# A decoder layer on one Trainium2 core: norm chains spread by a share set by stage, one product of the seven moved first, and the last walk of the weights backwards

## Chip, cores and metric

One core of one Trainium2 chip. The metric is device time per launch in microseconds (us), the median of several runs. TensorE is called PE, VectorE DVE, ScalarE ACT, GpSimd POOL and SyncE SP, as in the profile.

## The reference, cut to what matters

One decoder layer runs over 1024 prompt tokens and 8 x 4 decode tokens, D = 1024, FFN width 2816:

```python
h = _rms(x, n_mix_pre)
z = h @ w_in                      # q, k, v, pooling input
a, k_state, v_state = attn_fn(q, k, v)        # window of 128 keys, sinks
m, pool_state = _pool_mixer(u, pool_prev, pos0, w_pool, pool_scale)
mix = jnp.concatenate([a, m], axis=-1) @ w_out
x = x + _rms(mix, n_mix_post)
f = _rms(x, n_ffn_pre)
f = (jax.nn.silu(f @ w_gate) * (f @ w_up)) @ w_down
x = x + _rms(f, n_ffn_post)
x = x + jax.nn.sigmoid(x @ w_ple_gate) * (p @ w_ple)
```

All of it is float32. The outputs are the new x of both token sets and the key, value and pooling states.

## The kernel before, in words

**Layout.** The 1056 tokens lie in three groups g = 0, 1, 2 of 352 columns; features lie on the 128 partitions, so D is eight chunks of 128, kept as two halves of four chunks (128x1408). A float32 product is done as three matmuls on high and low halves: `split` (L145 to L147) makes the high half with a cast on ACT and the low half (the names ending in l: wl, fl, sl, and the second half of hid and pl) with a subtraction on DVE; `gemm` (L248) multiplies high by high, high by low and low by high. All matmuls are issued by L117.

**Weights.** `w_load` (L151) fetches a weight tile through SP's queue into one of three raw buffers (wr), and `w_split` (L162) splits it into one of four pairs of tiles (wh, wl). A raw buffer is free when its low half is made, a pair when its last matmul has read it. `need` (L232) keeps up to five items ahead in a list, ITEMS, that is planned beforehand.

**The walk over the FFN.** The 22 chunks of the FFN width are taken as 11 slabs of two. WALK (L191) has 16 steps n: slabs 0 to 4 with group 2 alone, slabs 5 to 10 with all groups, slabs 0 to 4 again with groups 0 and 1 (steps 11 to 15). `gate_up` (L806) makes one chunk of silu(f·gate)·(f·up). Group 2 takes a direct product of 24 matmuls for gate and for up. Groups 0 and 1 share seven products of 12 matmuls instead of eight, in Strassen's manner: two with the gate weights and sums of x (B11, B21), then S2·T2, S3·T3, a quarter of the up weights times T4, S1·T1, S4·B22. The S are sums of the weights, made by `w_sums` (L780): four additions on POOL (L790) in place in the two raw buffers, after their own splits, and then a split of the results into sh and sl. `downs` (L921) multiplies a slab's hidden activations (hid) by the down weights, six matmuls an output, and is called after the first product or products of the next step.

**The norm chains.** What a norm needs is written as generators: `ffn_steps` (L700) for the norm behind the mixing sub-layer and the one ahead of the FFN, `ple_steps` (L894) for the norm behind the FFN, both with `rstd_steps` (L264), whose two small matmul groups sum the squares over the partitions (acc) and broadcast the reciprocal root (dg). Each yields a load, the matmuls' worth of DVE work in the piece, and a wait. `turn` (L678), called after each product, counts the matmuls issued and lets a chain go on to its next piece when its time has come; the next time is DVE's planned time plus load/share, share = 0.45. A smaller share spreads the pieces over more matmuls. `chain` starts a chain after a wait, `finish` runs chains to their end.

**What orders the engines.** From L755 PE's instructions keep the order in which they are written, chains' matmuls included. The other engines' order is made by the tile scheduler, so a piece that is emitted later need not stand later on DVE.

**The end.** `ple_out` (L938) makes one output chunk m of one group: 6 matmuls with the projection w_ple and 24 with w_ple_gate, a sigmoid, a product and a sum, then the store. Group 2 does m = 0 and 1 (FIRST = 2) ahead of the last slab's down products of groups 0 and 1, and m = 2 to 7 behind them; then a second walk over m = 0 to 7 does groups 0 and 1, and all weights are fetched and split again. `plan_ple` (L219) plans both walks.

Of the kernel before, what the change touches and what calls it, by code (L numbers as in the profile page):

```python
# [16 lines left out]
P = 128  # L17
D = 1024
KC = D // P
# [39 lines left out]
def trunk_kernel(  # L59
# [61 lines left out]
    def bank():  # L121
        return psum.tile([P, 512], F32, tag="b", name=nm("b"))
# [39 lines left out]
    def w_split(j):  # L162
        if j >= len(plan) or j in pairs:
            return
        w_load(j)
        shape = plan[j][1]
        hi, lo = w_tile(shape, "wh"), w_tile(shape, "wl")
        split(hi, lo, raws[j])
        pairs[j] = (hi, lo)
# [7 lines left out]
    def add_plan(src, shape):  # L177
        plan.append((src, shape))
        return len(plan) - 1
# [16 lines left out]
    def item(kind, *js):  # L196
        ITEMS.append((kind, js))
        return len(ITEMS) - 1

    def direct_item(src, shape):  # L200
        return item("direct", add_plan(src, shape))
# [15 lines left out]
    WPE = [[], []]  # L217

    def plan_ple(n, m):  # L219
        wp = direct_item(w_ple[m // 4], [P, 2, 512]) if m % 4 == 0 else WPE[n][-1][0]  # L220
        WPE[n].append((wp, direct_item(w_pg[m], [P, KC, P])))

    FIRST = 2
    for m in range(FIRST):
        plan_ple(0, m)
    WD[-1] = [direct_item(w_dn[WALK[-1][0], j], [P, SLAB, 512]) for j in range(2)]
    for m in range(FIRST, KC):
        plan_ple(0, m)
    for m in range(KC):
        plan_ple(1, m)  # L230

    made = {}  # L232

    def need(k, ahead=LOOK):

        for i in range(len(made), min(k + ahead + 1, len(ITEMS))):
            kind, js = ITEMS[i]
            if kind == "direct":
                w_split(js[0])
                made[i] = pairs[js[0]]  # L240
            else:
                made[i] = w_sums(*(raws[ITEMS[j][1][0]] for j in js))
            for kind, js in ITEMS[i + 1 : i + 3]:
                if kind == "direct":
                    w_load(js[0])
        return made[k]
# [61 lines left out]
    def bc4(r):  # L308
        return r.unsqueeze(1).to_broadcast([P, 4, r.shape[1]])
# [39 lines left out]
    n = 4 * NDEC * PST  # L349
# [83 lines left out]
    for c in range(4):  # L433
        n = NDEC * DSEQ
# [240 lines left out]
    now, dve = [0.0], [0.0]  # L675
    chains = []

    def turn(n, share=0.45):  # L678

        now[0] += n  # L680
        for ch in list(chains):
            while ch in chains and ch[1] <= now[0]:
                try:
                    load, wait = next(ch[0])
                except StopIteration:
                    chains.remove(ch)
                    break
                dve[0] = max(dve[0], now[0]) + load / share
                ch[1] = dve[0] + wait

    def chain(steps, wait=0):
        chains.append([steps, now[0] + wait])

    def finish(ch_list):
        for ch in ch_list:
            for _ in ch[0]:
                pass
            chains.remove(ch)

    def ffn_steps(g):  # L700

        r = yield from rstd_steps(acc[g])
        for yh, xh in zip(ys[g], x1[g]):
            ve.tensor_tensor(yh, yh, bc4(r), op=ALU.mult)
            ve.tensor_tensor(xh, xh, yh, op=ALU.add)
            se.activation(yh, xh, AF.Square)
            yield 20, 0
        yield 0, 13
        acc2 = sum_halves(ys[g], g)
        yield 20, 6  # L710
        r = yield from rstd_steps(acc2)
        for h in range(2):
            nc.sync.dma_start(x1d[g][h], x1[g][h])
            for c in range(4):
                k = 4 * h + c
                ve.scalar_tensor_tensor(  # L716
                    ys[g][h][:, c, :], x1[g][h][:, c, :], gn[:, 2, k : k + 1], r, op0=ALU.mult, op1=ALU.mult
                )
            yield 14, 0
            if (g, h) == (1, 0):  # L720
                t_sum("T1")
                yield 20, 0
            else:
                op = f_operand(ys[g][h], g)
                yield 10, 0
                if g == 2:
                    fs[2].append(op)
                else:
                    f7[f"B{h + 1}{g + 1}"] = op
        if g == 1:  # L730
            for name in ("T3", "T2", "T4"):
                t_sum(name)
                yield 20, 0
# [8 lines left out]
    f7 = {}  # L742
# [10 lines left out]
        f7[name] = f_operand(out, 0)  # L753

    pinned[0] = True  # L755
    chain(ffn_steps(2), 19)
    for m in range(4):
        for g in (0, 1):
            out_attn(m, g)
# [10 lines left out]
        turn(24)  # L770
    chain(ffn_steps(1), 19)
    finish(chains[:-2])


    hid = [None] * G
# [27 lines left out]
    def quarter(w, h):  # L803
        return tuple(t[:, 4 * h : 4 * h + 4, :] for t in w)

    def gate_up(items, slot, gs, pending):  # L806

        ig, iu, is_ = items
        n = N

        def product(w, x):
            ps = bank()
            gemm(ps[:, :n], ops4(w, x))
            turn(12)
            return ps[:, :n]

        def direct(w):
            ps = bank()
            gemm(ps[:, :n], ops8(w, fs[2]))
            turn(24)  # L820
            return ps[:, :n]

        def add(out, a, ps):
            ve.tensor_tensor(out, a, ps, op=ALU.add)

        wg = need(ig)
        if 0 in gs:
            p1 = tmp(n, "p1")
            se.copy(p1, product(quarter(wg, 0), f7["B11"]))
        if 2 in gs:  # L830
            sl = tmp(n, "sl")
            se.activation(sl, direct(wg), AF.Silu)
        if 0 in gs:
            c11 = tmp(n, "c11")
            add(c11, p1, product(quarter(wg, 1), f7["B21"]))
            se.activation(c11, c11, AF.Silu)
        if pending:
            pending()
        for g in gs:
            if slot == 0:  # L840
                hid[g] = half(g, F32R, "hid")
        wu = need(iu)
        if 2 in gs:
            ve.tensor_tensor(sl, sl, direct(wu), op=ALU.mult)
            hid_put(2, slot, sl)
        if 0 not in gs:
            return
        s = need(is_)
        add(p1, p1, product(s["S2"], f7["T2"]))
        u3 = tmp(n, "u3")  # L850
        add(u3, p1, product(s["S3"], f7["T3"]))
        c21 = tmp(n, "c21")
        add(c21, u3, product(quarter(wu, 1), f7["T4"]))
        ve.tensor_tensor(c21, c21, c11, op=ALU.mult)
        hid_put(0, slot, c21)
        p5 = product(s["S1"], f7["T1"])
        add(u3, u3, p5)
        add(p1, p1, p5)
        add(p1, p1, product(s["S4"], f7["B22"]))
        se.activation(p1, p1, AF.Silu)  # L860
        ve.tensor_tensor(u3, u3, p1, op=ALU.mult)
        hid_put(1, slot, u3)
# [31 lines left out]
    def ple_steps(g):  # L894

        pl = half(g, F32R, "pl")
        pls[g] = pl[:, 0:2, :], pl[:, 2:4, :]
        for k in range(2):
            pr = tmp(NS[g], "pr")
            nc.sync.dma_start(pr, p[:, k, OFF[g] : OFF[g + 1]])  # L900
            split(pl[:, k, :], pl[:, 2 + k, :], pr)
        x2s[g] = []
        for h in range(2):
            x2[g][h] = half(g, s="x2")
            nc.sync.dma_start(x2[g][h], x1d[g][h])
        r = yield from rstd_steps(acc3[g])
        for h in range(2):
            yh, xh = os_[g][h], x2[g][h]
            ve.tensor_tensor(yh, yh, bc4(r), op=ALU.mult)
            for c in range(4):  # L910
                k = 4 * h + c
                ve.scalar_tensor_tensor(  # L912
                    xh[:, c, :], yh[:, c, :], gn[:, 3, k : k + 1], xh[:, c, :], op0=ALU.mult, op1=ALU.add
                )
            yield 24, 0
            x2s[g].append(f_operand(xh, g))
            yield 10, 0
# [3 lines left out]
    def downs(n):  # L921
        s, gs = WALK[n]
        for m in range(KC):
            for g in (2, 0, 1):
                if g in gs:
                    (last_down if g == 2 and s == NSLAB - 1 else down)(n, m, g)
        if s == NSLAB - 1:
            chain(ple_steps(2), 19)

    for n, (s, gs) in enumerate(WALK):  # L930
        if n == AHEAD:
            finish(list(chains))
        for i in range(SLAB):
            gate_up(WGU[n][i], i, gs, (lambda: downs(n - 1)) if i == 0 and n else None)
    finish(list(chains))


    def ple_out(n, m, g):  # L938
# [15 lines left out]

    for m in range(FIRST):
        ple_out(0, m, 2)
# [5 lines left out]
    chain(ple_steps(1), 19)  # L962
    for m in range(FIRST, KC):
        ple_out(0, m, 2)
    finish(chains[:1])
    for m in range(KC):
        for g in (0, 1):
            if g == 1 and m == 0:
                finish(list(chains))
            ple_out(1, m, g)  # L970

# [86 lines left out]
```

## Time and profile before

| | before |
|---|---|
| median of 3 runs | 1228.29 us (1227.34 to 1229.78) |
| the profiled execution | 1225.98 us |
| its span (first to last instruction) | 1223.9 us |
| mean granted clock of PE | 0.971 |
| PE busy | 1147.9 us (94%) |
| DVE busy | 741.7 us (61%) |
| ACT busy | 433.3 us (35%) |
| POOL busy | 187.1 us (15%) |

The span is one execution, and all durations come from it. Busy shares are averages over stages with different limits. A wait is put down to the engine that released it last; the granted clock is that which the throttle left to PE.

### The profile page before, as it was taken

How to read it: one execution, taken by the hardware profiler on the slowest of the kernel's cores; microseconds unless marked ns; L12 is line 12 of the kernel's file. 1: busy time of each engine (PE TensorE's matmuls, PEld its weight loads, DVE VectorE, ACT ScalarE, POOL GpSimd, SP SyncE). 2: the span in 40 equal slices, each digit the busy share in tenths (PEclk: the TensorE clock that was granted, in tenths of full speed). 3: DMA queues.
4: the chain of work that ended last, by engine and by line, in shares of the span. 5: the costliest groups of instructions: out<-in, count | busy, mean ns of one | idle time of the engine just before them, and what ended most of it. 6: DMA issues, size and time to landing. Idle time of an engine off the chain costs nothing.

```text
span 1223.9 us, 17417 instructions
## 1 busy us (share of the span) xinstructions
PE 1147.9 (94%) x7099; PEld 1109.0 (91%) x7099; DVE 741.7 (61%) x1161; ACT 433.3 (35%) x755; POOL 187.1 (15%) x150
## 2 busy tenths in 40 slices
PE   4699999999889999999999999999969999999898
PEld 3599986779889999999999999999969999999798
DVE  6644245676487894534555555547866576679542
ACT  4222035656345552433131313123423223355220
POOL 3344012110000003102021111111112213200000
PEclk9599999999989999999999999999979999999899
DMA  6211130036235331202121211213212122246321
GB/s 231 67 35 47 52 115 18 18 114 217 69 139 167 131 120 35 73 32 70 35 70 35 63 41 35 70 35 99 81 52 69 41 98 70 64 132 245 105 70 42
DMA packets 35104, 101.11 MB, mean 83 GB/s; under 512 B 4148, under 2 KB 14676, under 8 KB 35024
## 3 DMA queue, kind: packets, MB, share of 16 engines
q1 hardware_dynamic: 33264, 98.22, 23.7%
q10 hardware_dynamic: 1760, 1.78, 0.5%
q8 instruction: 56, 0.92, 0.3%
q14 instruction: 24, 0.20, 0.1%
HBM read 89.87 MB, written 10.11 MB: 82 GB/s over the span
## 4 chain that ended last, share of the span: by engine, by line
PE 83%; DVE 8%; POOL 3%; ACT 3%; DMA 1%; issue 1%; POOLq 0%; SPq 0%; DVEq 0%; ACTq 0%
PE b L117 79%; POOL wr L790 3%; DVE wl L147 2%; PE b L541 1%; PE b L509 1%; DMA xr<-in_x_dram 1%; ACT wh L146 1%; DVE h L324 1%; DVE sl L147 1%; ACT a L483 1%; ACT sh L146 1%; DVE fl L147 1%; DVE y L716 0%; PE b L588 0%; DVE x L912 0%
## 5 line engine op out<-in xcount | busy, mean ns | idle before, releaser
L117 PE MATMUL b<-fh,wh 128*128 128x352 f32 x808 | 263.9, 327 | 10.8 <-ACT fh L146 10.8
L117 PE MATMUL b<-hid,wh 128*128 128x352 f32 x1056 | 255.7, 324 | 10.7 <-ACT hid L146 8.0
L117 PE MATMUL b<-fl,wh 128*128 128x352 f32 x808 | 261.4, 324 | 3.3 <-DVE fl L147 3.3
L146 ACT CAST wh<-wr 128x1024 fp32r<-128x1024 f32 x140 | 146.6, 1049 | 332.0 <-PE b L117 273.5
L117 PE MATMUL b<-fh,wl 128*128 128x352 f32 x808 | 261.2, 323 | 0.0
L147 DVE TENSOR_TENSOR wl<-wr,wh 128x1024 fp32r<-128x1024 f32 x140 | 176.7, 1263 | 65.9 <-ACT wh L146 65.7
L117 PEld LDWEIGHTS b<-hid,wh 128*128 128x128 f32 x1056 | 184.2, 189 | 13.0 <-ACT hid L146 8.8
L117 PE MATMUL b<-hid,wl 128*128 128x352 f32 x528 | 170.1, 322 | 0.0
L790 POOL TENSOR_TENSOR wr<-wr 128x512 f32<-128x512 f32 x44 | 60.3, 1370 | 682.9 <-DVE wl L147 482.0
L117 PEld LDWEIGHTS b<-fh,wh 128*128 128x128 f32 x808 | 153.1, 190 | 12.0 <-ACT fh L146 11.7
L117 PEld LDWEIGHTS b<-fl,wh 128*128 128x128 f32 x808 | 153.5, 190 | 4.8 <-DVE fl L147 4.4
L117 PEld LDWEIGHTS b<-fh,wl 128*128 128x128 f32 x808 | 153.4, 190 | 0.0
L880 DVE TENSOR_TENSOR o<-o,b 128x352 f32<-128x352 f32 x240 | 116.0, 515 | 43.0 <-PE b L117 42.9
L117 PE MATMUL b<-h,wh 128*128 128x352 f32 x480 | 123.7, 340 | 18.6 <-ACT wh L146 9.7
L117 PE MATMUL b<-fh,sh 128*128 128x352 f32 x352 | 114.8, 326 | 6.6 <-ACT sh L146 6.6
L117 PE MATMUL b<-fh,sl 128*128 128x352 f32 x352 | 114.0, 324 | 3.3 <-DVE sl L147 3.3
L117 PE MATMUL b<-fl,sh 128*128 128x352 f32 x352 | 113.5, 322 | 0.0
L117 PEld LDWEIGHTS b<-h,wh 128*128 128x128 f32 x480 | 88.5, 199 | 21.8 <-ACT wh L146 9.7
L147 DVE TENSOR_TENSOR sl<-wr,sh 128x1024 fp32r<-128x1024 f32 x44 | 53.7, 1223 | 85.8 <-ACT sh L146 85.8
L146 ACT CAST sh<-wr 128x1024 fp32r<-128x1024 f32 x44 | 45.9, 1045 | 152.3 <-POOL wr L790 109.1
L117 PEld LDWEIGHTS b<-hid,wl 128*128 128x128 f32 x528 | 99.8, 189 | 0.0
L117 PE MATMUL b<-h,wl 128*128 128x352 f32 x240 | 80.3, 335 | 2.5 <-DVE wl L147 2.5
(156 smaller groups left out, 1601.4 us busy)
## 6 DMA issues: line engine op xcount, KB each, us to landing
wr<-in_w_gu_dram SPq DMA_DIRECT2D x64, 512.0 KB, 3.2
wr<-in_w_dn_dram SPq DMA_DIRECT2D x32, 512.0 KB, 3.4
wr<-in_w_pg_dram SPq DMA_DIRECT2D x16, 512.0 KB, 3.9
wr<-in_w_in_dram SPq DMA_DIRECT2D x10, 512.0 KB, 3.3
xr<-in_x_dram SPq DMA_DIRECT2D x6, 704.0 KB, 5.2
x<-in_x_dram SPq DMA_DIRECT2D x6, 704.0 KB, 9.4
x1d<-x SPq DMA_DIRECT2D x6, 704.0 KB, 3.5
x<-x1d SPq DMA_DIRECT2D x6, 704.0 KB, 5.6
```

The lines of the kernel that those rows point to most:

```text
L117: ins = te.matmul(*args, **kw)
L146: se.copy(hi, src)
L147: ve.tensor_tensor(lo, src, hi.bitcast(F32), op=ALU.subtract)
L324: ve.scalar_tensor_tensor(lo[:, c, :], xr[:, c, :], gc, hi[:, c, :].bitcast(F32), op0=ALU.mult, op1=ALU.subtract)
L483: se.activation(t[:, c, :], t[:, c, :], AF.Exp, bias=nmx[:, c : c + 1], scale=scale, accum_out=sm[:, c : c + 1])
L509: te.matmul(which[kv][:, c * WIN : (c + 1) * WIN], qT[c][rows, b * WIN : (b + 1) * WIN], kT[rows, at * WIN : (at + 1) * WIN], start=True, ...
L541: te.matmul(o[64 * kv : 64 * kv + 64, :], vtok[:, at, 64 * kv : 64 * kv + 64], pt[:, 4 * kv : 4 * kv + 4, :], start=n == 0, stop=n == len( ...
L790: ge.tensor_tensor(out, a, b, op=op)
L880: ve.tensor_tensor(o, o, v, op=ALU.add)
```

## The change

- **Share by stage.** The share becomes a cell that is set as the program goes on: 0.6 from the first chain until groups 0 and 1 have left the output projection (it was 0.45), 0.45 in the FFN, 0.1 when group 2's per-layer chain starts (behind the down products of slab 10), 0.7 for the chains of groups 0 and 1 at the end. Group 2's FFN chain starts 8 matmuls after it is due instead of 19.
- **T4.** In walk steps 11 to 15 the product with T4 is issued ahead of S2 and S3, and added where it was.
- **The end.** FIRST is 1. The second walk runs m = 7 to 0 and reuses the pairs of m = 7 and 6, and of w_ple's second half, that the first walk left: three loads and three splits fewer. The `finish` in it moves to m = 7.

```diff
--- before.py
+++ after.py
@@ -220,14 +220,19 @@
         wp = direct_item(w_ple[m // 4], [P, 2, 512]) if m % 4 == 0 else WPE[n][-1][0]
         WPE[n].append((wp, direct_item(w_pg[m], [P, KC, P])))
 
-    FIRST = 2
+    FIRST = 1
     for m in range(FIRST):
         plan_ple(0, m)
     WD[-1] = [direct_item(w_dn[WALK[-1][0], j], [P, SLAB, 512]) for j in range(2)]
     for m in range(FIRST, KC):
         plan_ple(0, m)
-    for m in range(KC):
-        plan_ple(1, m)
+
+    WPE[1] = [None] * 6 + WPE[0][6:]
+    wp = WPE[0][-1][0]
+    for m in reversed(range(6)):
+        if m == 3:
+            wp = direct_item(w_ple[0], [P, 2, 512])
+        WPE[1][m] = wp, direct_item(w_pg[m], [P, KC, P])
 
     made = {}
 
@@ -675,7 +680,9 @@
     now, dve = [0.0], [0.0]
     chains = []
 
-    def turn(n, share=0.45):
+    share = [0.6]
+
+    def turn(n):
 
         now[0] += n
         for ch in list(chains):
@@ -685,7 +692,7 @@
                 except StopIteration:
                     chains.remove(ch)
                     break
-                dve[0] = max(dve[0], now[0]) + load / share
+                dve[0] = max(dve[0], now[0]) + load / share[0]
                 ch[1] = dve[0] + wait
 
     def chain(steps, wait=0):
@@ -753,7 +760,7 @@
         f7[name] = f_operand(out, 0)
 
     pinned[0] = True
-    chain(ffn_steps(2), 19)
+    chain(ffn_steps(2), 8)
     for m in range(4):
         for g in (0, 1):
             out_attn(m, g)
@@ -770,6 +777,7 @@
         turn(24)
     chain(ffn_steps(1), 19)
     finish(chains[:-2])
+    share[0] = 0.45
 
 
     hid = [None] * G
@@ -845,12 +853,16 @@
             hid_put(2, slot, sl)
         if 0 not in gs:
             return
+        if 2 not in gs:
+            p4 = product(quarter(wu, 1), f7["T4"])
         s = need(is_)
         add(p1, p1, product(s["S2"], f7["T2"]))
         u3 = tmp(n, "u3")
         add(u3, p1, product(s["S3"], f7["T3"]))
         c21 = tmp(n, "c21")
-        add(c21, u3, product(quarter(wu, 1), f7["T4"]))
+        if 2 in gs:
+            p4 = product(quarter(wu, 1), f7["T4"])
+        add(c21, u3, p4)
         ve.tensor_tensor(c21, c21, c11, op=ALU.mult)
         hid_put(0, slot, c21)
         p5 = product(s["S1"], f7["T1"])
@@ -925,6 +937,7 @@
                 if g in gs:
                     (last_down if g == 2 and s == NSLAB - 1 else down)(n, m, g)
         if s == NSLAB - 1:
+            share[0] = 0.1
             chain(ple_steps(2), 19)
 
     for n, (s, gs) in enumerate(WALK):
@@ -933,6 +946,7 @@
         for i in range(SLAB):
             gate_up(WGU[n][i], i, gs, (lambda: downs(n - 1)) if i == 0 and n else None)
     finish(list(chains))
+    share[0] = 0.7
 
 
     def ple_out(n, m, g):
@@ -963,9 +977,9 @@
     for m in range(FIRST, KC):
         ple_out(0, m, 2)
     finish(chains[:1])
-    for m in range(KC):
+    for m in reversed(range(KC)):
         for g in (0, 1):
-            if g == 1 and m == 0:
+            if g == 1 and m == KC - 1:
                 finish(list(chains))
             ple_out(1, m, g)
```

On DVE, where group 2 enters the FFN: acc are sums of squares, wl a weight's low half, L704 and L705 (L711 and L712 in the changed kernel) are group 0's y·r and x+y, L716 (L723) group 2's scalings y<-x,c,b, and fl are the low halves of group 2's normalised x, first half and second. Before:

```order
L608 TENSOR_TENSOR acc_1303<-acc_1303,sq_2809 128x352
L147 TENSOR_TENSOR wl_2813<-wr_2736,wh_2812 128x1024
L705 TENSOR_TENSOR x_2326<-x_2326,y_1266 128x1408
L716 SCALAR_TENSOR_TENSOR y_1268<-x_2322,c_72,b_2823 128x352 x4
L716 SCALAR_TENSOR_TENSOR y_2188<-x_2324,c_72,b_2823 128x352 x3
L147 TENSOR_TENSOR fl_2831<-y_1268,fh_2830 128x1408
L716 SCALAR_TENSOR_TENSOR y_2188<-x_2324,c_72,b_2823 128x352
L704 TENSOR_TENSOR y_2532<-y_2532,b_2818 128x1408
L147 TENSOR_TENSOR fl_2840<-y_2188,fh_2839 128x1408
L705 TENSOR_TENSOR x_2328<-x_2328,y_2532 128x1408
```

After:

```order
L723 SCALAR_TENSOR_TENSOR y_1268<-x_2322,c_72,b_2748 128x352 x3
L723 SCALAR_TENSOR_TENSOR y_2188<-x_2324,c_72,b_2748 128x352 x2
L147 TENSOR_TENSOR wl_2785<-wr_2701,wh_2784 128x1024
L613 TENSOR_TENSOR acc_1303<-acc_1303,sq_2781 128x352
L711 TENSOR_TENSOR y_1266<-y_1266,b_2794 128x1408
L147 TENSOR_TENSOR fl_2791<-y_1268,fh_2790 128x1408
L712 TENSOR_TENSOR x_2326<-x_2326,y_1266 128x1408
L613 TENSOR_TENSOR acc_1303<-acc_1303,sq_2825 128x352
L147 TENSOR_TENSOR wl_2829<-wr_2746,wh_2828 128x1024
L723 SCALAR_TENSOR_TENSOR y_2188<-x_2324,c_72,b_2748 128x352 x2
L711 TENSOR_TENSOR y_2535<-y_2535,b_2794 128x1408
L147 TENSOR_TENSOR fl_2840<-y_2188,fh_2839 128x1408
```

Six of group 2's eight scalings (one of them stands above these rows) and its first fl have moved ahead of x+y; y·r stays ahead of the first fl, and the second fl stays behind both pieces of group 0.

On DVE, in walk step 11, where two chunks' weights pass through the raw buffers: wl are low halves of weights and sl of weight sums, L824 (L832) sums of products, L861 (L873) u·p, L909 (L921) group 2's o·r and L912 (L924) its residual updates. wl_7728 (wl_7721) frees the raw buffer for the next gate or up weights. Before:

```order
L147 TENSOR_TENSOR sl_7606<-wr_7337,sh_7605 128x1024
L912 SCALAR_TENSOR_TENSOR x_7654<-o_3042,c_72,x_7654 128x352 x2
L147 TENSOR_TENSOR wl_7612<-wr_7485,wh_7611 128x1024
L912 SCALAR_TENSOR_TENSOR x_7654<-o_3042,c_72,x_7654 128x352 x2
L824 TENSOR_TENSOR p_7339<-p_7339,b_7702 128x352
L824 TENSOR_TENSOR c_7748<-p_7733,b_7749 128x352
L909 TENSOR_TENSOR o_3043<-o_3043,b_7715 128x1408
L861 TENSOR_TENSOR u_7631<-u_7631,p_7339 128x352
L824 TENSOR_TENSOR p_7733<-p_7733,b_7774 128x352
L912 SCALAR_TENSOR_TENSOR x_7656<-o_3043,c_72,x_7656 128x352
L147 TENSOR_TENSOR wl_7728<-wr_7609,wh_7727 128x1024
```

After:

```order
L147 TENSOR_TENSOR sl_7606<-wr_7337,sh_7605 128x1024
L873 TENSOR_TENSOR u_7667<-u_7667,p_7339 128x352
L832 TENSOR_TENSOR c_7741<-p_7726,b_7742 128x352
L147 TENSOR_TENSOR hid_7596<-u_7667,hid_7596 128x352
L147 TENSOR_TENSOR wl_7625<-wr_7485,wh_7624 128x1024
L921 TENSOR_TENSOR o_3042<-o_3042,b_7774 128x1408
L147 TENSOR_TENSOR wl_7721<-wr_7609,wh_7720 128x1024
L924 SCALAR_TENSOR_TENSOR x_7652<-o_3042,c_72,x_7652 128x352 x4
```

Of group 2's chain, both o·r and five updates stood ahead of wl_7728; one o·r stands ahead of wl_7721, and the updates behind it.

On DVE, some ten rows further in the same step, where the hid of group 1 (hid_7596) is finished ahead of the step's down products; L880 (L892) are sums of down products. Before:

```order
L912 SCALAR_TENSOR_TENSOR x_7656<-o_3043,c_72,x_7656 128x352 x2
L824 TENSOR_TENSOR p_7733<-p_7733,b_7840 128x352
L147 TENSOR_TENSOR sl_7868<-wr_7485,sh_7867 128x1024
L824 TENSOR_TENSOR c_7892<-p_7877,b_7893 128x352
L861 TENSOR_TENSOR u_7788<-u_7788,p_7733 128x352
L880 TENSOR_TENSOR o_4477<-o_4477,b_7912 128x352
L147 TENSOR_TENSOR fl_7952<-x_7656,fh_7951 128x1408
L147 TENSOR_TENSOR hid_7596<-u_7788,hid_7596 128x352
```

After:

```order
L147 TENSOR_TENSOR hid_7595<-c_7816,hid_7595 128x352
L832 TENSOR_TENSOR p_7726<-p_7726,b_7836 128x352
L147 TENSOR_TENSOR sl_7859<-wr_7485,sh_7858 128x1024
L873 TENSOR_TENSOR u_7801<-u_7801,p_7726 128x352
L832 TENSOR_TENSOR c_7883<-p_7868,b_7884 128x352
L892 TENSOR_TENSOR o_4477<-o_4477,b_7903 128x352
L147 TENSOR_TENSOR hid_7596<-u_7801,hid_7596 128x352
L924 SCALAR_TENSOR_TENSOR x_7654<-o_3043,c_72,x_7654 128x352 x2
```

Group 2's last fl and its last two updates stood ahead of hid_7596; the updates now stand behind it and the fl further on. sl still stands ahead of u·p and hid_7596.

## The prediction

> **What bounds the kernel now.** I read the page first, for the shares of the chain that ended last:
>
> ```profile
> span 1223.9 us, 17417 instructions
> ...
> PE 83%; DVE 8%; POOL 3%; ACT 3%; DMA 1%; issue 1%; POOLq 0%; SPq 0%; DVEq 0%; ACTq 0%
> ```
>
> TensorE (PE) sets the pace for 83% of the span. The change takes out no matmul, so it can only shorten the other 17%, about 208 us; much of that lies in the first 300 us, which the diff doesn't touch. So the question is where PE waits in the parts that it does touch. The waits of PE from 860 us to the end (total us, times, longest):
>
> ```profile
> PE b L117 <- ACT hid L146: 8.0, 2, 6.1
> PE b L117 <- ACT sh L146: 6.6, 5, 1.4
> PE b L117 <- DVE sl L147: 3.3, 5, 0.7
> PE b L117 <- ACT fh L146: 3.2, 1, 3.2
> PE b L117 <- DVE fl L147: 2.3, 2, 1.2
> PE b L117 <- DVE hid L147: 1.6, 2, 1.2
> ```
>
> Twenty-five microseconds of waits, of three kinds: for the hidden activations (hid), for the weight sums of GpSimd (sh, sl), and for normalised activations (fh, fl). Busy times by stage show where they lie (length; PE, PEld, DVE, ACT and POOL busy with counts; granted clock; DMA share; GB/s):
>
> ```profile
> 330.00:345.00 15.00, 6.41 (x25) 5.26 (x24) 13.13 (x16) 5.96 (x6) 0.00 (x0) 0.74 0.32 118
> 342.00:346.00 4.00, 4.00 (x14) 3.88 (x15) 4.00 (x4) 1.37 (x1) 0.00 (x0) 0.50 0.00 0
> 640.00:863.00 223.00, 223.00 (x1409) 223.00 (x1408) 129.52 (x223) 58.73 (x88) 37.26 (x28) 1.00 0.17 56
> 863.00:901.00 38.00, 26.77 (x151) 24.48 (x149) 32.37 (x42) 16.35 (x21) 11.22 (x8) 0.86 0.21 70
> 1012.00:1056.00 44.00, 41.90 (x262) 41.31 (x261) 28.87 (x48) 14.18 (x20) 10.64 (x8) 1.00 0.22 72
> 1132.00:1150.00 18.00, 12.41 (x67) 11.48 (x67) 14.17 (x19) 4.50 (x5) 0.00 (x0) 0.89 0.40 128
> ```
>
> The third row is the yardstick: undisturbed, a matmul takes 223.00/1409 = 0.158 us, a product of 12 takes 1.9 us, one of 24 takes 3.8 us. Against it, each disturbed stretch loses its length less its count times 0.158. **A** (330 to 345, where group 2 enters the FFN) loses 15.0 − 25×0.158 = 11.0 us; **B** (863 to 901, where group 2 leaves it, walk step 11) loses 38.0 − 151×0.158 = 14.1; **C** (1132 to 1150, where groups 0 and 1 enter the per-layer products) loses 18.0 − 67×0.158 = 7.4. In A and B VectorE (DVE) is busy 13.13 of 15 and 32.37 of 38 us: there it is the bound. The row of walk step 14 (1012 to 1056) has PE idle for 44.0 − 41.9 = 2.1 us at full clock, with DVE busy only 66%: a fourth place, **T4**, a latency and not a load.
>
> **The change part by part.**
>
> *A: share 0.6 and first wait 8.* The chain of waits through A (start, us, what) and two PE rows, the broadcasts of both groups' scales and what follows the first FFN product:
>
> ```profile
> 331.96 1.62 DVE y L704
> ...
> 336.69 3.44 DVE y L716 x7
> ...
> 341.76 8.35 PE b L117 x38
> ```
>
> ```profile
> 331.17 1.35 PE L117 MATMUL b<-dg,c 88*128 88x352 f32 x4
> ...
> 348.18 0.71 PE L117 MATMUL b<-c,acc 128*88 128x1 f32 x8
> ```
>
> Before, both broadcasts stand at 331.17, and DVE then does group 0's y·r and x+y ahead of group 2's seven scalings of 3.44/7 = 0.49 us. After, by the order, group 2's broadcast stands 48 matmuls earlier (331.17 − 7.6 = 323.6) and group 0's 24 earlier (327.4), so six of the eight scalings fit beside the last output projections. Laid out in the new order: from 328.1 a weight's low half 1.2, a sum of squares 0.4, y·r 1.6 and group 2's first low half 1.6 end at about 333.6, with 0.7 for what they wait for; PE is there at 332.2. Then x+y 1.6, the sum 0.4, a weight 1.2, two scalings 1.0, y·r 1.6 and the second low half 1.6 end at 340.9. The 12 matmuls that need it take 1.9 us at full clock, 12×4.00/14 = 3.4 at the halved clock of the second window row. So the product ends between 342.8 and 344.3, and with five more slow matmuls behind it (0.6) A gains 5.4 to 3.3 us. Between its operands PE still stalls for 1.4, 3.7 and 1.6 us. The window rows have the clock halved after 8 us of idleness and at 1.00 through 2.1 us: 3.7 lies between, and I take −4.3. From this I take off 1.1 (two scalings, as DVE, not PE, paces the first hid too): **A −3.2**. Bounds: −2, if more of DVE's queue moves up with it, and −9, if the scheduler's other order lets both halves pass.
>
> [...]
>
> *B: share 0.1 for group 2's per-layer chain.* The chain there:
>
> ```profile
> 883.36 3.35 DMA wr<-in_w_gu_dram
> ...
> 887.86 1.24 DVE wl L147
> ...
> 896.30 1.23 DVE sl L147
> ...
> 898.92 1.53 DVE fl L147
> ...
> 900.94 4.14 PE b L117 x16
> ```
>
> A raw weight buffer is free only at 883.3, since the low half that frees it stands in DVE's queue behind group 2's residual updates; the transfer, its split, four sums on GpSimd (889.1 to 895.2) and theirs follow, then group 2's fl (1.53) still stands ahead of the last hid. After, the order puts that fl behind the hid, and the freeing low half behind one o·r instead of two and five updates. But the share does not do all it says: the scheduler still puts both o·r (L921) and six of the eight updates ahead of the sums. Laid out: buffer free 877.8, transfer done 881.2, split done 885.0 (−4.1 against 889.1, since updates stand between), sums 890.8, their split 893.0, u·p and hid 894.9 against 900.9: **B −6.0**. The stall does not go, because sl waits for GpSimd ahead of u·p and hid in DVE's in-order queue. Bounds: −3 (two updates and the sum's split later than laid out) to −10 (the split done with the transfer at 882).
>
> *T4 first, in steps 11 to 15.* Chain of step 13 around its second chunk:
>
> ```profile
> 966.91 1.07 ACT wh L146
> ...
> 976.05 1.24 DVE sl L147
> ...
> 977.33 2.82 PE b L117 x16
> ```
>
> The split of the next up weights starts when T4's pair is read, and from 966.91 to 977.29 runs split, four sums and their split: 10.4 us. Before, T4 is third of seven products, so S1, S4 and the two gate products, 4×1.9 = 7.6 us, cover it; the lack is 2.1 to 2.8 us. After, T4 is first: its pair is free two products earlier, and six products and the next T4 lie ahead of the next S2, 7×1.9 = 13.3 us. I add 1.0 for the transfers and DVE work that now meet it, 11.4, and the stall goes with 1.9 to spare. T4 itself then needs only the split (2.4 of 6×1.9 = 11.4 us), and its bank is held two products longer, of eight. The sh and sl waits total 6.6 + 3.3 = 9.9 in five places, one of them in B (about 1.5): **T4 −8.4**, bounds −6 and −9.9. In the first chunk of a step 16 down products of six cover everything, before and after.
>
> *C: FIRST 1 and the walk backwards.* Of the waits, 3.2 + 2.3 = 5.5 us are here, for groups 0 and 1's split x; the rest of the 7.4 is clock. FIRST = 1 puts 30 more matmuls, 4.7 us, between group 0's last down product and its first per-layer product. Backwards, the pairs of m = 7 and 6 and of w_ple's second half are still split: three transfers, three casts and three low halves of 1.24 us fewer, 3.7 us of DVE where it is busy 14.17 of 18 us. 4.7 + 3.7 = 8.4 against 5.5. Laid out in DVE's new order, the tightest, group 1's second half, ends 0.8 us ahead of its need. **C −7.4**, bounds −4 (one half late by 1.5 us, its clock too) and −8.5. The queue of SP loses three loads and no store moves behind a load that waits; the last matmul's group, (m = 0, g = 1), has the same tail as before.
>
> *Nothing:* the share of 0.45 in steps 0 to 10, where DVE is busy 129.52 of 223 us; 0.7 at the end, which the 4.7 us cover.
>
> **Sum:** −3.2 − 6.0 − 8.4 − 7.4 = −25.0 us. The profiled execution took 1225.98, its span 1223.9, so 2.1 lie around the span and stay. The median of the runs, 1228.29, is 2.3 above it; I carry the sum over: 1228.3 − 25.0 = **1203 us**, in a profiled span of about 1199.
>
> **The rivals.**
>
> *R1: A and B only move.* Both are DVE's load (13.13 of 15, 32.37 of 38); an order that adds no idle DVE time can shift the stall to the next hid. For: no DVE operation leaves either place. Against: in both, the chain holds DVE work that PE doesn't need then (x+y, fl). Gain T4 and C alone, 15.8: about 1212.
>
> *R2: A and B vanish,* as 1.00 clock and enough cover would give: 11.0 + 14.1 + 8.4 + 7.4 = 40.9, about 1187. For: six of eight scalings done early. Against: the laid-out queue still has 6 us behind them.
>
> *R3: slower.* Steps 11 to 15 now run GpSimd's sums beside other DVE work. Two DVE rows of one form, alone and beside a sum:
>
> ```profile
> 875.24 1.07 DVE L912 SCALAR_TENSOR_TENSOR x<-o,c,x 128x352 f32<-128x352 f32 x2
> ...
> 890.97 3.10 DVE L912 SCALAR_TENSOR_TENSOR x<-o,c,x 128x352 f32<-128x352 f32 x2
> ```
>
> Beside sums two updates take 2.0 us more. If the sums' chain grows likewise, it decides from 13.3 us on, and only in the five second chunks. To end at +3 it has to eat 28, 5.6 in each, so the chain must be 18.9 instead of 10.4, four such pairs in every chunk: about 1231. [...]
>
> **How the numbers follow.** The forecast (A and B partly, T4 and C wholly) gets 0.68; R1 0.17, since A and B rest on a laid-out queue; R2 0.10; R3 0.03; 0.02 for sums that cancel within 0.2%, 2.5 us, about what a measurement of this kernel can tell from no change. Faster 0.68 + 0.17 + 0.10 = 0.95, same 0.02, slower 0.03. The forecast's own bounds: 2 + 3 + 6 + 4 = 15 (1213) to 9 + 10 + 9.9 + 8.5 = 37 (1191), ends that won't all meet. R1's 1212 is within; R2 and R3 are left out, so the range is 1191 to 1213.
>
> **What would show it.** In the profile after: A, the first fh wait near 3.7 instead of 7.6 us and the acc product at 343 to 345; B, the hid wait of 6.1 shrunk but there, and the first down product's end near 895; T4, no sh or sl wait after step 11, and steps of 45 us down to about 43; C, no fh or fl wait in the second per-layer walk, clock 1.00, three wl fewer. Wrong would be: sums of 2 us or more on GpSimd with sh waits back (R3); hid waits as long as before at new places (R1); or hid waits gone (R2).

## The result and the profile after

The changed kernel takes 1198.77 us (median of 4 runs, 1198.22 to 1199.91), the kernel before in the same comparison 1228.85 (1227.34 to 1229.78): a ratio of 0.9758, 95% interval 0.9741 to 0.9774. The forecast was 1203 us in a range of 1191 to 1213. The profiled execution of the changed kernel spans 1196.4 us, 27.5 less than before, where the sum said 25.0.

The page of the changed kernel, its span and its chain:

```profile
span 1196.4 us, 17405 instructions
...
PE 87%; DVE 7%; ACT 2%; issue 1%; DMA 1%; POOL 1%; SPq 0%; DVEq 0%; POOLq 0%; ACTq 0%
```

PE's share of the chain rose from 83% to 87%, and POOL's fell from 3% to 1%: of the weight sums, only those of step 11 are still on it. All waits of PE from 860 us to the end, where there were six groups and 25 us:

```profile
PE b L117 <- ACT hid L146: 6.1, 2, 3.4
PE b L117 <- DVE hid L147: 1.3, 3, 0.6
```

The waits for sh, sl, fh and fl are gone, those for hid are not. The stages, rows that answer to those of before:

```profile
342.00:346.00 4.00, 4.00 (x19) 3.97 (x19) 2.56 (x3) 2.55 (x3) 0.00 (x0) 0.50 0.47 183
346.00:350.00 4.00, 4.00 (x15) 4.00 (x15) 2.63 (x5) 0.14 (x1) 0.00 (x0) 0.50 0.40 132
862.00:896.00 34.00, 27.23 (x157) 25.82 (x156) 29.16 (x41) 12.70 (x18) 9.92 (x8) 0.91 0.24 78
1003.00:1046.00 43.00, 43.00 (x272) 43.00 (x271) 31.28 (x50) 14.84 (x20) 12.10 (x9) 1.00 0.23 74
1110.00:1130.00 20.00, 20.00 (x127) 20.00 (x126) 13.77 (x19) 5.08 (x8) 0.00 (x0) 1.00 0.24 86
```

The last two rows have PE busy without a gap from step 14 into step 15, and around the head of the second per-layer walk. The third still has stalls of 6.8 us in all in step 11. The first two show the clock halved, at 0.50, for at least 8 us where group 2 enters the FFN: A's gain was cut there.

Where the 27.5 us came from is read between marks that stand in both traces. Before: the broadcast of group 1's scale some 76 matmuls behind the first FFN product, the start of the products with sums and T4 in step 11, the same in step 12, and the start of the last step's down products in the per-layer stage:

```profile
360.28 0.76 PE L117 MATMUL b<-dg,c 88*128 88x352 f32 x2
...
857.25 0.32 PE L117 MATMUL b<-fh,sh 128*128 128x352 f32 x1
...
916.04 0.32 PE L117 MATMUL b<-fh,sh 128*128 128x352 f32 x1
...
1086.96 0.48 PE L117 MATMUL b<-hid,wh 128*128 128x352 f32 x2
```

After, the same places:

```profile
359.54 0.76 PE L117 MATMUL b<-dg,c 88*128 88x352 f32 x2
...
856.36 0.32 PE L117 MATMUL b<-fh,wh 128*128 128x352 f32 x1
...
909.07 0.32 PE L117 MATMUL b<-fh,wh 128*128 128x352 f32 x1
...
1063.82 0.48 PE L117 MATMUL b<-hid,wh 128*128 128x352 f32 x2
```

| stretch | before | after | difference | forecast |
|---|---|---|---|---|
| A: from the start to the second mark | 857.25 | 856.36 | −0.9 | −3.2 |
| B: between the second and third marks | 58.8 | 52.7 | −6.1 | −6.0 |
| T4: from there to the last mark, steps 12 to 15 | 170.9 | 154.75 | −11.4 | −8.4 |
| C: from the last mark to the span's end | 136.9 | 132.6 | −9.1 | −7.4 |

30 matmuls (4.8 us) moved from the third stretch to the fourth with FIRST = 1; the differences have them taken out. The sum is −27.5. Of it, 7.5 us are PE's own busy time, 1147.9 us before and 1140.4 after for the same 7099 matmuls: fewer of them ran at a halved clock (mean granted clock 0.971 before, 0.98 after). So the prediction's opening, that only the 17% of the chain outside PE could be shortened, was too narrow; its own terms already counted lost clock. The medians are 30.1 apart; the profiled execution of before, 1225.98, was under its median.

### The profile page after: what moved, and what is told of

Same layout as the page of the kernel before. It is cut to its first block, busy times and chain, and to the rows that moved or that the text cites. A ratio compares the mean times of both kernels' runs of the same rounds, so it can differ in the third digit from the quotient of the medians.

```text
span 1196.4 us, 17405 instructions
## 1 busy us (share of the span) xinstructions
PE 1140.4 (95%) x7099; PEld 1105.4 (92%) x7099; DVE 741.9 (62%) x1158; ACT 430.1 (36%) x752; POOL 188.5 (16%) x150
## 4 chain that ended last, share of the span: by engine, by line
PE 87%; DVE 7%; ACT 2%; issue 1%; DMA 1%; POOL 1%; SPq 0%; DVEq 0%; POOLq 0%; ACTq 0%
PE b L117 83%; DVE wl L147 2%; PE b L546 1%; PE b L514 1%; DMA xr<-in_x_dram 1%; DVE h L329 1%; ACT a L488 1%; POOL wr L798 0%; PE b L593 0%; DVE a L539 0%; ACT wh L146 0%; DVE dg L282 0%; POOL a L494 0%; DVE mx L480 0%; DVE acc L613 0%
## 5 line engine op out<-in xcount | busy, mean ns | idle before, releaser
L146 ACT CAST wh<-wr 128x1024 fp32r<-128x1024 f32 x137 | 143.3, 1048 | 303.7 <-PE b L117 259.1
L147 DVE TENSOR_TENSOR wl<-wr,wh 128x1024 fp32r<-128x1024 f32 x137 | 173.1, 1265 | 62.9 <-ACT wh L146 62.6
L892 DVE TENSOR_TENSOR o<-o,b 128x352 f32<-128x352 f32 x240 | 116.5, 517 | 43.6 <-PE b L117 43.4
L146 ACT CAST sh<-wr 128x1024 fp32r<-128x1024 f32 x44 | 45.7, 1047 | 132.6 <-POOL wr L798 82.0
```

Of the source, the lines that this page charges most:

```text
L146: se.copy(hi, src)
L147: ve.tensor_tensor(lo, src, hi.bitcast(F32), op=ALU.subtract)
L892: ve.tensor_tensor(o, o, v, op=ALU.add)
```

## The experiments

Each traced run is read between the same marks. In four of the traces (the share of 0.1 alone, FIRST alone, backwards alone, and the late per-layer chain) PE's undisturbed stretch before step 11 ran 6 us slower than in the others (shown at the end), so medians of single parts say less than the marks, which lie behind most of it. The diffs show the lines that matter; `...` stands for lines left out.

**T4 alone, on the kernel before.** The edit:

```diff
+        if 2 not in gs:
+            p4 = product(quarter(wu, 1), f7["T4"])
         s = need(is_)
...
-        add(c21, u3, product(quarter(wu, 1), f7["T4"]))
+        if 2 in gs:
+            p4 = product(quarter(wu, 1), f7["T4"])
+        add(c21, u3, p4)
```

> The kernel before with T4 alone moved first in steps 11 to 15. Theory (places are independent; T4's order alone removes the sums' lateness): steps 12 to 14 fall from 45.0, 44.7 and 44.6 us to 42.6 to 42.0, no sh or sl wait is left after step 11, and the span is 10 to 12 us shorter than before. Rival 1 (the sums came in time because the share of 0.1 spread group 2's chain, which left VectorE freer): less than 4 us. Rival 2 (the sums only just fit and meet more VectorE work): sh waits of 0.5 us or more stay in the second chunks, 5 to 8 us.

1211.27 us, 0.9849 of the kernel before (0.9811 to 0.9886). Its marks and its waits of PE from 858 to 1125 us:

```profile
858.67 0.32 PE L117 MATMUL b<-fh,wh 128*128 128x352 f32 x1
...
914.23 0.32 PE L117 MATMUL b<-fh,wh 128*128 128x352 f32 x1
...
1074.69 0.48 PE L117 MATMUL b<-hid,wh 128*128 128x352 f32 x2
```

```profile
PE b L117 <- ACT hid L146: 6.7, 2, 3.4
PE b L117 <- DVE hid L147: 1.8, 2, 1.2
```

Steps 12 to 15 take 160.5 instead of 170.9 us, −10.4, with no sh or sl wait: the first theory. Step 13 takes 42.5 us here and the changed kernel's step 14 takes 42.0, both without a wait and with the same work; this run had come to the slower pace by then, so by estimate some 2 us more over the four steps would be T4's. What no theory had said: step 11 falls from 58.8 to 55.6, with the share still 0.45, and its longest hid wait from 6.1 to 3.4. Half of B's gain is T4's.

**The share of 0.1 alone, on the kernel before.**

```diff
-    def turn(n, share=0.45):
+    share = [0.45]
+
+    def turn(n):
...
         if s == NSLAB - 1:
+            share[0] = 0.1
             chain(ple_steps(2), 19)
```

> The kernel before with the share of 0.1 for group 2's per-layer chain alone. Theory (B's gain is VectorE's queue, reordered by the spread chain): the hid wait of 6.1 us in step 11 falls to about 3.4, span 5 to 7 us shorter. Rival (B's gain comes from T4 standing first in step 11, whose pair and raw buffer are free 3.8 us earlier): span at most 2 us shorter, and a hid wait of 5 us or more stays.

1226.94 us, ratio 0.9985 (0.9954 to 1.0016): no difference that can be measured. The marks and the wait:

```profile
863.23 0.32 PE L117 MATMUL b<-fh,sh 128*128 128x352 f32 x1
...
903.83 0.66 PE L117 MATMUL b<-hid,wh 128*128 128x352 f32 x1 [6.24 <-ACT hid L146]
...
921.39 0.32 PE L117 MATMUL b<-fh,sh 128*128 128x352 f32 x1
```

58.2 us for step 11 instead of 58.8, and the long wait stays: the rival was right. The slower pace of this run is worth some 0.6 us here (276 matmuls at 0.160 instead of 0.158 us), so the share alone gives 1.2 us at most where the weight sums are late by T4's place.

**The share of 0.45 again, on the changed kernel** (the line share[0] = 0.1 taken out).

> The changed kernel with group 2's per-layer chain at a share of 0.45 again; all else as changed. Theory (with T4 first, step 11 is bound by VectorE's queue, so the spread counts now, though alone it counted nothing): from the start of step 11 to the end of its down products 55 to 56 us instead of 52.7, span 2.5 to 3.5 us longer than the changed kernel's. Rival (all of B came from T4's order): 52.2 to 53.4 us, span the same.

Step 11's marks, and the wait in it:

```profile
855.83 0.32 PE L117 MATMUL b<-fh,wh 128*128 128x352 f32 x1
...
893.98 0.66 PE L117 MATMUL b<-hid,wh 128*128 128x352 f32 x1 [3.36 <-ACT hid L146]
...
911.30 0.32 PE L117 MATMUL b<-fh,wh 128*128 128x352 f32 x1
```

Step 11 takes 55.5 us instead of 52.7: as the theory said, with T4 first the share is worth 2.8 us there. But steps 12 to 15 take 153.5 us instead of 154.75, so 1.2 comes back, and the median is 1198.86 us (1198.03 to 1200.22) beside the changed kernel's 1198.77, from another comparison. The span is 1.0 longer, less than the theory's 2.5 to 3.5, and by the medians the share's net worth can't be told from nothing.

**The two halves of C, alone, on the kernel before:** FIRST = 1 with the forward walk, and the backward walk with FIRST = 2.

```diff
-    FIRST = 2
+    FIRST = 1
```

> The kernel before with FIRST = 1 alone; the second walk still runs forward and fetches everything again. Theory (30 more matmuls, 4.7 us, cover most of the 5.6 us of waits at the second walk's head, and the lack comes back as its own clock): 5 to 8 us shorter, a wait of up to 1 us left. Rival (the cover alone does all of C and the reuse nothing): 9 us shorter, no wait left.

```diff
-    for m in range(KC):
-        plan_ple(1, m)
+
+    WPE[1] = [None] * 6 + WPE[0][6:]
...
-    for m in range(KC):
+    for m in reversed(range(KC)):
...
```

> The kernel before with the second per-layer walk backwards and the reuse of three split weights alone; FIRST stays 2. Theory (three low halves, 3.7 us of VectorE, leave the queue ahead of the last fl): 3 to 6 us shorter, an fh or fl wait of 1 to 3 us left. Rival (VectorE's load is not what makes fl late, but the last down products are): at most 1 us shorter.

FIRST alone: 1223.98 us, ratio 0.9954 (0.9931 to 0.9977); backwards alone: 1225.76, ratio 0.9961 (0.9938 to 0.9984). The waits at the second walk's head, first of FIRST alone:

```profile
1150.66 0.42 PE L117 MATMUL b<-fh,wh 128*128 128x352 f32 x1 [1.81 <-ACT fh L146]
1152.33 0.43 PE L117 MATMUL b<-fl,wh 128*128 128x352 f32 x1 [1.24 <-DVE fl L147]
```

and of the walk backwards alone:

```profile
1149.18 0.43 PE L117 MATMUL b<-fh,wh 128*128 128x352 f32 x1 [1.23 <-ACT fh L146]
1150.84 0.43 PE L117 MATMUL b<-fl,wh 128*128 128x352 f32 x1 [1.23 <-DVE fl L147]
```

From the last stretch's first mark (1089.76 and 1093.59) to the span's end (1226.6 and 1225.6) they take 136.8 and 132.0 us; with the moved 4.8 taken out of the first, −4.9 and −4.9 against 136.9. Cover and load add up to 9.8, about the 9.1 of both together. That the two are equal is good to some 0.5 us: a product of 30 matmuls behind the waits takes 4.83 us in the first run, 4.77 in the second and 4.80 before. The theory's sizes hold for the second; the first gained 0.1 less and waited 2 us longer than said.

**A alone, on the kernel before:** the share of 0.6 and the wait of 8.

```diff
-    def turn(n, share=0.45):
+    share = [0.6]
+
+    def turn(n):
...
-    chain(ffn_steps(2), 19)
+    chain(ffn_steps(2), 8)
...
+    share[0] = 0.45
```

> The kernel before with the share of 0.6 up to the FFN and the first wait of 8 alone. Theory (the operands come as laid out, but the clock stays halved until ten us after the last stall, so the gain is lost): the second fl ends near 341.2 us instead of 345.3, but the second FFN norm's broadcast, 360.28 us before, comes only 0.5 to 1.2 us earlier, and the span is about 1 us shorter. Rival (the rest of A is lost to VectorE's later queue and not to the clock): PE waits of 2 us or more between 345 and 361.

1223.17 us, ratio 0.9972 (0.9952 to 0.9992). The stall of the changed kernel is there to the hundredth, but the clock behaves otherwise:

```profile
340.21 0.43 PE L117 MATMUL b<-fh,wh 128*128 128x352 f32 x1 [3.44 <-ACT fh L146]
```

```profile
342.00:346.00 4.00, 4.00 (x21) 4.00 (x22) 2.56 (x2) 2.22 (x2) 0.00 (x0) 0.65 0.46 179
346.00:350.00 4.00, 4.00 (x27) 4.00 (x26) 3.30 (x6) 0.72 (x3) 0.00 (x0) 1.00 0.37 116
```

The clock is back at 346 us; in the changed kernel's profile it was 0.50 to 350. So the broadcast (group 1's; the expectation calls it the second FFN norm's) comes at 357.19, 2.35 earlier than the changed kernel's 359.54, although this stall ended at 340.21 and the changed kernel's 0.67 earlier, at 339.54. Both theories are short here: VectorE's queue doesn't cost more later (the rival), but neither is the loss of the gain a fixed thing. The same waits cost 3 us more or less, by how long the clock stays halved. The other traces with this A and this stall (the share of 0.45, the pinned sums, the late per-layer chain and T4 second) have it halved for some 9 us from the end of the last wait, as the changed kernel has; A alone has 3.

**Work in the stall, on the changed kernel:** 22 matmuls with an unread result between the halves of the first FFN product.

```diff
+    filled = []
...
-            gemm(ps[:, :n], ops8(w, fs[2]))
+            ops = ops8(w, fs[2])
+            gemm(ps[:, :n], ops[:4], stop=False)
+            if not filled:
+                filled.append(bank())
+                for _ in range(22):
+                    mm(filled[0][:, :n], ops[0][0], ops[0][2], start=True, stop=True)
+            gemm(ps[:, :n], ops[4:], start=False)
```

> The changed kernel with 22 matmuls more, whose result nobody reads, between the two halves of the first FFN product, where PE waited 3.45 us for the second half. Theory (the granted clock falls because of that stall, and it is the halved clock that eats A's gain): the clock stays at 0.9 or more from 342 to 354, the broadcast at 359.54 comes 3 to 5 us earlier, the span is 3 to 5 us shorter than the changed kernel's although PE does 3.5 us more. Rival (the clock does not hang on this stall, or VectorE is the bound behind it): broadcast within 1 us of 359.5, span the same.

```profile
342.00:346.00 4.00, 4.00 (x30) 4.00 (x30) 2.55 (x2) 2.48 (x3) 0.00 (x0) 1.00 0.45 180
```

```profile
355.90 0.76 PE L117 MATMUL b<-dg,c 88*128 88x352 f32 x2
```

The clock stays at 1.00, where the changed kernel's row has 0.50, and the broadcast comes 3.6 us earlier: 1195.31 us (1194.03 to 1195.50), beside 1198.22 of the pinned kernel below, which has the changed kernel's A and ran on the same chip. That this stall halved the clock here, and that the halved clock ate most of A's gain, is shown.

**Group 0's chain later, on the changed kernel.**

```diff
-    chain(ffn_steps(0), 19)
+    chain(ffn_steps(0), 110)
```

> The changed kernel with group 0's FFN chain started 110 matmuls after its squares instead of 19, so that its scalings and residual sums, 3 x 1.6 us of VectorE, stand behind both fl of group 2. Theory (A is bound by the order of VectorE's queue, not by its load): second fl ends near 336 instead of 341.2, PE stalls fall from 5.9 to about 2 us, the clock keeps at 0.8 or more from 338 to 350, and the span is 5 to 9 us shorter. Rival (VectorE's load is the bound; the work only moves): PE waits of the same length reappear at the next hid, span within 1.5 us of the changed kernel's.

1194.55 us (1194.09 to 1194.95), ratio to the kernel before 0.9738 (0.9703 to 0.9774).

```profile
336.92 0.43 PE L117 MATMUL b<-fl,wh 128*128 128x352 f32 x1 [1.23 <-DVE fl L147]
...
359.54 0.43 PE L117 MATMUL b<-hid,wh 128*128 128x352 f32 x1 [2.19 <-ACT hid L146]
360.71 0.43 PE L117 MATMUL b<-hid,wh 128*128 128x352 f32 x1 [0.74 <-DVE hid L147]
```

The stalls for fh and fl fall from 5.9 to 2.0 us and the clock stays at 1.00, as the theory had it, but 2.9 us reappear at the next hid, behind the y·r and x+y that now stand there, as the rival had it. Step 11 begins at 851.8 instead of 856.4, 4.6 us earlier, but takes 54.0 us instead of 52.7, and the span is 3.2 us shorter: between the theory's 5 to 9 and the rival's 1.5.

**The sums pinned behind hid, on the changed kernel:** the casts and low halves of step 12's first weight sums are issued behind all that is written before them.

```diff
-        se.copy(hi, src)
-        ve.tensor_tensor(lo, src, hi.bitcast(F32), op=ALU.subtract)
+        both = se.copy(hi, src), ve.tensor_tensor(lo, src, hi.bitcast(F32), op=ALU.subtract)
+        if pin:
+            for ins in both:
+                tc.keep_in_program_order(ins)
...
-            split(*hl, src)
+            split(*hl, src, pin=len(sums) == 15)
```

> The changed kernel with the casts and low halves of step 12's first weight sums pinned behind all that is written before them on ScalarE and VectorE, so that group 1's last hid of step 11 no longer stands behind them. Theory (B's rest is sl waiting for GpSimd ahead of hid in VectorE's queue): the hid wait of 3.4 us at 893.2 falls to 1 us or less, hid's low half ends near 891 instead of 893.9, span 2.5 to 4.5 us shorter. Rival (VectorE's load in step 11 is the bound): hid within 0.7 us of 893.9 and span the same.

1198.22 us (1196.58 to 1199.13), no gain: the span is 1196.7 us beside the changed kernel's 1196.4. The hid wait of 3.4 us falls to 1.1 (the other one, 2.7, stays), but step 11 gains 1.3 us only (51.4), and it began 1.6 us later. The chain shows what came in sl's place:

```profile
891.62 0.43 DVE u L878
892.05 0.99 DVE x L929 x2
893.04 0.45 DVE hid L146
```

Group 2's last two updates slipped into the gap, ahead of hid, which neither theory had. But the rival's signs came true, hid's low half at 893.5 and the span the same, and its cause too: with sl out of the way, the chain is VectorE's work without a gap from 883.4 us to this hid.

**Group 2's per-layer chain later, on the changed kernel; and all three together.**

```diff
-            chain(ple_steps(2), 19)
+            chain(ple_steps(2), 250)
```

> The changed kernel with group 2's per-layer chain started 250 matmuls after its squares instead of 19, so that none of it meets step 11. Theory (what is left of B is group 2's updates in VectorE's queue, first ahead of the weights' low halves, then ahead of hid): the hid waits of 2.7 and 3.4 us fall to 1 us or less in all, 52.7 us become 43 to 46, span 7 to 10 us shorter. Rival (GpSimd's sums are the bound, group 2's chain only fills VectorE's gaps): the wait of 3 us for hid stays, span at most 2 us shorter.

> The changed kernel with group 0's FFN chain 110 matmuls late, group 2's per-layer chain 250 late, and step 12's first weight sums pinned behind hid. Theory (the stalls are separate): late_g0's 4 us and late_ple's 7 to 10 add up, the pin brings nothing more; 1183 to 1188 us. Rival (late work piles up on VectorE in steps 12 to 15 and at the end): 1190 us or more, with new waits after 920 us.

The late chain alone: 1203.08 us (two runs at 1200.5 to 1200.7, two at 1205.5 to 1206.9, the traced one among these), ratio 0.9792 (0.9759 to 0.9825), not faster than the changed kernel. Step 11's start, step 12's start, step 12's waits and step 13's start:

```profile
862.60 0.32 PE L117 MATMUL b<-fh,wh 128*128 128x352 f32 x1
...
905.80 0.32 PE L117 MATMUL b<-fh,wh 128*128 128x352 f32 x1
...
937.66 0.61 PE L117 MATMUL b<-hid,wh 128*128 128x352 f32 x1 [3.55 <-ACT hid L146]
...
943.08 1.44 PE L117 MATMUL b<-hid,wh 128*128 128x352 f32 x2 [2.59 <-ACT hid L146]
...
959.67 0.32 PE L117 MATMUL b<-fh,wh 128*128 128x352 f32 x1
```

Step 11 falls to 43.2 us, inside the theory's 43 to 46, and step 12 grows from 42.6 to 53.9: the stall went along with the chain, and the two steps take 1.8 us more in all than in the changed kernel (some 1.2 of it by this run's slower pace). All three together: 1199.81 us (1194.77 to 1202.42), with the same pair of waits in step 12 (3.85 and 2.59), so nothing above the late group 0 alone; the profiled run spans 1193.0 us and that one's 1193.2. The rival was right: late work piles up where it falls.

**T4 second, on the changed kernel:** S2, T4, S3.

```diff
+        s = need(is_)
+        add(p1, p1, product(s["S2"], f7["T2"]))
         if 2 not in gs:
             p4 = product(quarter(wu, 1), f7["T4"])
-        s = need(is_)
-        add(p1, p1, product(s["S2"], f7["T2"]))
```

> The changed kernel with T4 between S2 and S3 instead of ahead of both. Theory (each product that T4 stands later takes 1.9 us of the sums' cover: 11.4 us are left for a chain of 10.6): sh and sl waits of 0 to 0.5 us a chunk, steps 13 and 14 at 42.6 to 43.1 us, span at most 2 us longer than the changed kernel's. Rival (it is the first place itself that counts, since S2 is what waits): sh waits of over 1 us are back in every second chunk, span 5 us longer.

1204.81 us (1203.82 to 1205.84), ratio 0.9813 (0.9790 to 0.9836), some 6 us more than the changed kernel. In step 13:

```profile
968.75 0.43 PE L117 MATMUL b<-fh,sl 128*128 128x352 f32 x1 [0.63 <-DVE sl L147]
...
984.66 0.43 PE L117 MATMUL b<-hid,wh 128*128 128x352 f32 x1 [0.58 <-DVE hid L147]
```

sh is in time and sl 0.63 late, so the chain needs about 12.0 us where 11.4 were covered; steps 13 and 14 take 44.1 and 43.3 us instead of 42.6 and 42.0. The theory's mechanism holds, its size does not: the pair freed 1.9 us later also puts the next weight's low half ahead of u·p and hid on VectorE, which is the second row, and steps 12 to 15 take 160.1 us in all, 5.3 more. The rival's price came near, without its waits for sh.

## Why the prediction was right, point by point

**The sum** was 25.0 for 27.5, with two terms too small, one too large and one right for a reason that was only partly its own. That it came within 2.5 is in part luck: T4 and C gave 4.7 more than said, A 2.3 less.

**T4, −8.4, was −11.4.** The step was the price: the sh and sl waits were added up, and what they cost besides was taken at nothing. In step 15 the kernel before had lost clock too. The stretch 1056 to 1101 of its trace loses 45.0 − 263 × 0.158 = 3.4 us, of which 2.1 are waits:

```profile
1056.00:1101.00 45.00, 42.90 (x263) 42.31 (x262) 31.80 (x54) 22.39 (x33) 5.31 (x4) 0.96 0.35 110
```

The 22 matmuls behind the sl wait took 5.2 us there and 3.6 to 3.7 in steps 12 to 14, so 1.5 of the missing 3.0 are step 15's clock; the rest is spread over the steps and was not traced further. By the yardstick, length less count times 0.158, as for A, B and C, the four steps lost 170.9 − 998 × 0.158 = 13.2 us, and the changed kernel still loses 154.75 − 968 × 0.158 = 1.8. The cover was right: 13.3 us were enough and 11.4 were not, by T4 first and second. R3's longer sums did not come: sums beside VectorE took 5.8 us in step 13 (956.1 to 961.9), 5.6 before.

**C, −7.4, was −9.1:** no wait is left, as forecast; the halved clock behind the waits (0.50 from 1148 to 1152 us) was left out of the loss. The three products of 30 matmuls that the waits touch take 6.3, 11.35 and 5.7 us before, and 4.8 each undisturbed there: a loss of 8.9 in all. Cover and load are worth about 4.9 each, where the prediction had 4.7 and 3.7.

**A, −3.2, was −0.9.** The laid-out queue was right to 0.3 us: 340.9 was forecast for the end of the second low half, and the chain has it at 341.2:

```profile
332.38 1.62 DVE fl L147
...
339.55 1.61 DVE fl L147
...
341.21 6.89 PE b L117 x26
```

The sign named for A came true as well: the acc product behind the first FFN product stands at 344.60, 3.6 us ahead of the 348.18 of before.

```profile
344.60 1.23 PE L117 MATMUL b<-c,acc 128*88 128x1 f32 x8
```

What failed is the step "with five more slow matmuls behind it". From the acc product to the broadcast PE does the same work in both traces without a wait, in 360.28 − 348.18 = 12.1 us before and 359.54 − 344.60 = 14.9 after: 2.8 of the 3.6 are lost again to the halved clock, which lasted until some 350 us, where 0.6 had been priced. Taking −4.3, midway between the full clock's −5.4 and the halved clock's −3.3, was 1.0 too hopeful besides. Against both stands the 1.1 taken off for the first hid, which did not come: PE's wait there is 0.33 us after and 0.34 before. Filling the stall showed the cause, and the run of A alone showed that it could as well have been 3 us better.

**B, −6.0, was −6.1, and the reason given was half wrong.** The size came from the order of the whole changed kernel, which held T4's move too; the prediction put it down to the share of 0.1. Alone the share gives 0.6 us (1.2 at most), T4 alone 3.2, the share on top of T4 another 2.8, of which 1.2 is lost again in steps 12 to 15. That the stall would stay with sl ahead of hid was right as far as it went: pinned, the wait fell from 3.4 to 1.1, and then VectorE's full queue, group 2's updates in it, stood there.

**The rivals.** R1, that stalls at A and B only move, was wrong for B; at A its number nearly came out, for another reason, the clock. It was right for the next change: a chain taken out of step 11 altogether makes the same stall in step 12. That the scheduler packs a chain's pieces together, whatever the share, was in the prediction (both o·r and six of eight updates ahead of the sums), and the late start did not spread them either: in its step 12 both o·r and six of the eight updates stand within some 17 us. R2's vanished stalls did not come, with 5.9 us of them left at A and 7.4 from step 11 on.

## What to carry to other kernels

Time a stretch by its length less its count of matmuls at the undisturbed rate, not by adding up the waits: what a stall does to the clock is in the first and not in the second (8.9 us against 5.5 of waits in C here). Where several edits share a stage, lay out the order without each of them before one is credited; and a chain of side work that stalls PE in one step can do the same in the next, where it is moved whole. Whether keeping its pieces apart would avoid that was not tried. Where a chain waits for a buffer to be read, issue the product that reads it last earlier: here one product's place was worth more than all shares.

## What the runs showed of the hardware

- After a stall of 3.4 to 3.5 us in A, the granted clock fell to 0.50; with work put into that stall, so that PE was idle for 0.62 us of 334 to 338 and 1.24 of 338 to 342, it stayed at 1.00. But a short stall was not free everywhere: in step 15 of the kernel before, waits of 1.44 and 0.67 us were followed by matmuls at 0.29 us from 1067.8 to 1071.0 (granted clock 0.59 in 1067 to 1071), while much the same pair in each of steps 12 to 14 left the clock at 1.00. The prediction had read the 2.1 us of one step as harmless. The rows of A alone and of the changed kernel have the same stalls, and the clock was back at 346 us in the one and still at 0.50 until 350 in the other, with PE busy in all 8.00 us from 342 to 350; what made the two runs differ was not tested here.
- At a granted clock of 1.00 PE ran at two paces in these traces. The same undisturbed stretch, of the kernel before and then of FIRST alone, which has the same work there:

```profile
480.00:540.00 60.00, 60.00 (x380) 60.00 (x379) 26.75 (x41) 22.67 (x39) 10.65 (x8) 1.00 0.17 53
```

```profile
480.00:540.00 60.00, 60.00 (x375) 60.00 (x374) 25.59 (x40) 22.15 (x38) 10.66 (x8) 1.00 0.16 53
```

  0.158 us a matmul in the one and 0.160 in the other, over some 440 us from about 420 to the stall in step 11: 6 us. It came in executions of unlike kernels, and T4 alone changed to it in the midst of one, behind step 11 (0.158 us a matmul from 780 to 840 us, 0.160 from 1030 to 1060). The spread of the kernel before (1222.89 to 1235.03 us over 25 runs) would fit it, but the only trace of that kernel ran at 0.158 us there; what sets the pace stays open.
- Two residual updates of group 2 took 3.10 us beside GpSimd's sums and 1.07 alone, as the prediction had it; what slowed them was not tested. In the changed kernel GpSimd's sums meet VectorE's work in every step from 11 on, and in step 13 four of them took 5.8 us instead of 5.6.
